# Nine of eleven gate/up chunks as seven products, in two stretches, with two sums of weights added by the loads

## The chip, the core and the metric

The kernel runs on one core of a Trainium2 chip. The metric is the device time of one execution in microseconds (us). TensorE (PE) multiplies matrices, VectorE (DVE) and ScalarE (ACT) work elementwise, GpSimd (POOL) and SyncE (SP) here issue DMAs. Each engine runs its own instructions strictly in order and waits on semaphores for the others.

## The reference

One layer on 256 tokens with 2048 channels, all in float32: a SwiGLU feed-forward, a mixer, a second feed-forward, each followed by a layer norm, and an embedding gate at the end.

```python
def _swiglu(x, w1, w3, w2):
    return (jax.nn.silu(x @ w1) * (x @ w3)) @ w2
...
x = _layer_norm(ALPHA * x + 0.5 * _swiglu(x, ffn1_w1[i], ffn1_w3[i], ffn1_w2[i]), ln1_g[i], ln1_b[i])
mix = _hybrid_mixer(x, w_in[i], ...)
x = _layer_norm(ALPHA * x + mix, ln2_g[i], ln2_b[i])
x = _layer_norm(ALPHA * x + 0.5 * _swiglu(x, ffn2_w1[i], ffn2_w3[i], ffn2_w2[i]), ln3_g[i], ln3_b[i])
x = x + jax.nn.sigmoid(x @ w_ple_gate[i]) * (p[i] @ w_ple_proj[i])
```

w1 and w3 are 2048 x 5632, w2 is 5632 x 2048. The mixer projects x by a wide matrix w_in, runs an mLSTM and a stick-breaking attention, and merges them under gates.

## The kernel before

**Matmuls.** A weight is loaded as a raw float32 tile of 128 partitions x 2 x 512 (256 rows by 512 columns, 512 KB). It is split in two: `hi` is the value rounded to the float32r type (a cast on ACT, L1243), `lo` is the rest (a subtraction on DVE, L1247). Activations are split in the same way. A unit is one split weight against one tile of 128 tokens: for each of the two blocks of 128 rows three matmuls of 512 columns, hi x hi, hi x lo and lo x hi (L1294 to L1296), six in all. They add up in one of eight PSUM banks; when the last unit of a sum has run, a function `done` or `add` evacuates the bank.

**Chunks.** The 5632 hidden columns are eleven chunks of 512. A plain chunk (`up`) has eight weights of w1 and eight of w3, each used by two units (the two token tiles). A chunk by `up7` goes through `seven`, a scheme of Strassen's kind: for each quad of 512 rows of the contraction, the activations form a 2 x 2 block matrix (two token tiles by two halves of the rows), and the weights another: B11 and B21 are the upper and lower half of the rows of w1, B12 and B22 those of w3. Seven products take the place of eight. M1 uses B11, M2 uses B21, M3 uses B22, M5 uses T1 = B11 + B12, M7 uses T3 = B12 + B22, M6 uses T2 = T1 + B22, M4 uses T4 = T2 + B21; the activations enter plainly or as sums that were made once (`act.forms`). Each product adds up over the four quads. Before the change, chunks 1, 2, 3, 5, 6, 7, 9 and 10 go this way, and 0, 4 and 8 plainly. All units of M1 run first, then all of M2 (each with its own load of B11 and B21), then for each quad M5, M7, M6, M4, M3. With `loaded` = 1, T1 is made by a load of B12 and an accumulating load of B11 into the same tile (issued by POOL, L1220), and T3 likewise in the last quad alone. The other sums are additions on DVE (L363).

In the mixer `both7` does the same for five pairs of column blocks of w_in, with `loaded` = 0: all sums on DVE.

**Order.** The program is a list of units. A main list (the plain chunks and the down passes, which multiply hidden chunks by w2 and add into the residual at L624) and a side list (the `up7` chunks) are merged by `weave` in proportion. From the list, weights are put in order of first use. `loads` issues raw loads on SP (L1215), at most 8 raw tiles held at once in the feed-forward (6 in the mixer's first part), and `split_one` splits a weight while at most 6 split weights are held. `make` puts the DVE additions shortly ahead of the split that needs them. An accumulating load's tile is moved three places ahead in the order of loads (AHEAD). Elementwise work after a product (`silu`, `late`, `turn`, which transposes hidden values for the down pass) is spawned with a delay counted in PE time. 48 pages of SBUF are shared by raw tiles, split tiles, activations and the residual.

Of the kernel before, what the change touches and what calls it, by code (L numbers as in the profile page):

```python
# [135 lines left out]
class Weight:  # L136


    def __init__(self, raw, loads, frees, make=None, after=None):
        self.raw, self.loads, self.frees, self.make, self.after = raw, loads, frees, make, after  # L140
        self.cols, self.uses, self.index, self.made = raw.cols, 0, None, False


class Unit:


    def __init__(self, tile, tt, acc, act, chunk, sub, start, stop, done):
        self.tile, self.cols, self.tt, self.acc = tile, tile.cols, tt, acc
        self.act, self.chunk, self.sub = act, chunk, sub
        self.start, self.stop, self.done = start, stop, done  # L150
        tile.uses += 1


# [34 lines left out]
def kernel(  # L188
# [159 lines left out]
    def seven(wa, ca, wb, cb, rows, cols, act, done, loaded):  # L348

        n = rows // (4 * P)
        accs = {m: {} for m in range(1, 8)}

        def unit(m, i, tile, src, half, sub):
            return Unit(tile, half, accs[m], src, i, sub, i == 0, i == n - 1, lambda ps, t, m=m: done(m, ps))

        def plus(out, a, b):
            def make():
                nc.vector.tensor_tensor(out=out.tile[:, :, :cols], in0=a.tile[:, :, :cols], in1=b.tile[:, :, :cols],  # L363
                                        op=ALU.add)
            return make

        units = []
        for m, sub in ((1, 0), (2, 2)):
            for i in range(n):
                units.append(unit(m, i, plain(rows_of(wa, (4 * i + sub) * P, ca, cols)), act, 0, sub))  # L370
        for i in range(n):
            b11, b12, b22, b21 = (rows_of(w, (4 * i + sub) * P, c, cols)
                                  for w, c, sub in ((wa, ca, 0), (wb, cb, 0), (wb, cb, 2), (wa, ca, 2)))
            by_load = loaded and i % loaded == 0
            if by_load:
                t1 = Raw(b12.src, cols, b11.src)
                first = Weight(t1, [t1], [])
            else:
                t1 = b11
                first = Weight(t1, [b11, b12], [], plus(b11, b11, b12))  # L380
            if loaded == 1 and i == n - 1:
                third = Weight(t3 := Raw(b12.src, cols, b22.src), [t3, b22], [t3])
            else:
                third = Weight(b12, [b12, b22] if by_load else [b22], [b12], plus(b12, b12, b22))
            units += [
                unit(5, i, first, act.forms, 0, 0),
                unit(7, i, third, act.forms, 1, 0),
                unit(6, i, Weight(t1, [], [], plus(t1, t1, b22), first), act.forms, 0, 2),
                unit(4, i, Weight(b21, [b21], [t1, b21], plus(b21, t1, b21)), act, 1, 2),
                unit(3, i, Weight(b22, [], [b22]), act.forms, 1, 2),  # L390
            ]
        return units

    def both7(w, ca, cb, act, dest, ready, loaded):

        r, held = {}, {}

        def put(k, t, a, b, op):
            nc.vector.tensor_tensor(out=r[k, t], in0=a, in1=b, op=op)

        def rest():
            u = r[0, 1]
            put(0, 1, held[7], u, ALU.add)
            z = r[1, 1] = dest(1, 1)
            nc.vector.scalar_tensor_tensor(out=z, in0=u, scalar=-1.0, in1=held[5],
                                           op0=ALU.mult, op1=ALU.subtract)
            ready(1, 1)
            return
            yield

        def done(m, ps):
            held[m] = ps
            if m == 1:
                r[0, 1] = dest(0, 1)
                nc.scalar.copy(r[0, 1], ps)
            elif m == 2:
                r[0, 0] = dest(0, 0)
                put(0, 0, ps, r[0, 1], ALU.add)
                ready(0, 0)
            elif m == 6:  # L420
                r[1, 0] = dest(1, 0)
                put(0, 1, ps, r[0, 1], ALU.add)
                put(1, 0, held[5], r[0, 1], ALU.add)
                sched.spawn(rest(), DELAY["rest"])
            elif m == 4:
                sched.until(lambda: (1, 1) in r)
                put(0, 1, ps, r[0, 1], ALU.add)
                ready(0, 1)
            elif m == 3:
                put(1, 0, ps, r[1, 0], ALU.subtract)  # L430
                ready(1, 0)

        return seven(w, ca, w, cb, D, COL, act, done, loaded)
# [110 lines left out]
    def ffn(w1, w3, w2, act, norm, skew=True, ahead=()):  # L544
# [22 lines left out]
        def up7(c):  # L567
            r, held = {}, {}

            def both(out, a, b, op):  # L570
                nc.vector.tensor_tensor(out=out, in0=a, in1=b, op=op)  # L571

            def done(m, ps):
                held[m] = ps
                if m == 1:
                    r["u"] = temp()
                    nc.scalar.copy(r["u"][:], ps)
                elif m == 2:
                    r["g0"] = temp()
                    both(r["g0"][:], ps, r["u"][:], ALU.add)  # L580
                    sched.spawn(silu(r["g0"]), DELAY["silu"])
                elif m == 6:
                    u, v, z = r["u"], temp(), temp()
                    both(u[:], ps, u[:], ALU.add)
                    both(v[:], held[5], u[:], ALU.add)
                    r["v"], r["z"] = v, z
                    sched.spawn(rest(), DELAY["rest"])
                elif m == 4:
                    sched.until(lambda: "rest" in r)
                    both(r["u"][:], ps, r["u"][:], ALU.add)  # L590
                    sched.spawn(silu(r["u"]), DELAY["silu"])
                elif m == 3:
                    both(r["v"][:], ps, r["v"][:], ALU.subtract)
                    sched.spawn(late(r["u"], r["v"], r["z"], r["g0"]), DELAY["late" if c < n - 1 else "last"])

            def rest():
                both(r["u"][:], held[7], r["u"][:], ALU.add)
# [466 lines left out]
    def ups(g, swap=False):  # L1064
# [3 lines left out]
            parts.reverse()  # L1068
        return parts[0] + parts[1]

    def gate_dest(g):
        def dest(k, t):
            if (g, t) not in gt:
                gt[g, t] = big()
            return gt[g, t][:, k * COL:(k + 1) * COL]
        return dest

    def pair(g):
        return both7(w_in, ga0 + g * COL, ga0 + D + g * COL, x1T, gate_dest(g), in_two(lambda t: gt[g, t], lambda k, t: ("gate", g, t, k)), 0)
# [6 lines left out]
    program.extend(weave(main, both7(w_in, sq0 + 2 * HS * DS, sq0 + 2 * HS * DS + COL, x1T, sv_dest, sv_ready, 0)  # L1086
                         + both7(w_in, 3072, 3072 + COL, x1T, mo_dest, mo_ready, 0) + pair(1) + pair(2) + pair(3)))
# [146 lines left out]
    def split_one():  # L1234
# [7 lines left out]
        for ks in pieces(j):  # L1242
# [3 lines left out]
                make(j + 2)  # L1246
            nc.vector.tensor_tensor(out=lo[:, ks], in0=r[:, ks], in1=hi[:, ks], op=ALU.subtract)  # L1247
# [28 lines left out]
    for u in program:  # L1276
# [14 lines left out]
        for k in range(2):  # L1291
            hi, lo = a[:, 0, u.sub + k], a[:, 1, u.sub + k]
            first, last = u.start and k == 0, u.stop and k == 1
            nc.tensor.matmul(ps, hi, w[0][:, k, :u.cols], start=first, stop=False)  # L1294
            nc.tensor.matmul(ps, hi, w[1][:, k, :u.cols], start=False, stop=False)  # L1295
            nc.tensor.matmul(ps, lo, w[0][:, k, :u.cols], start=False, stop=last)  # L1296
        sched.now += 6 * 0.2161 * u.cols / COL
        u.tile.uses -= 1
        if u.tile.uses == 0:
# [32 lines left out]
```

## Time and profile before

| | us |
|---|---|
| three runs | 2176.99, 2177.59, 2181.51 (median 2177.59) |
| the profiled execution, first to last instruction (span) | 2176.9 |

Stages of the profiled execution, about: 0 to 650 us first feed-forward and its norm, 700 to 1400 us mixer and second norm, 1400 to 2050 us second feed-forward, then the embedding gate. Busy share of the engines by slices of a fortieth of the span, in tenths, and what the DMA engines moved:

```profile
DVE  6899999999998799898988985799989999999874
ACT  7565665556664766667766563565656655656472
DMA  9899999899994666676878876589999999999743
GB/s 326 254 301 292 287 295 309 278 289 311 306 343 156 213 223 221 219 239 202 281 235 269 283 260 213 184 240 305 290 283 289 314 278 282 320 287 335 244 164 103
```

How to read it: a group's row names line, engine, operation, output and inputs, count, then busy time in us, the mean duration in ns, and the idle time of that engine just before these instructions with what ended it. PE's rows overlap each other, so the distance from start to start is what one matmul takes. A row of DMA issues gives the count, the size and the median time from issue to landing.

### The profile page before, as it was taken

The numbers are of one execution on the slowest core, as the hardware profiler recorded it, in microseconds if no ns is written. First come the engines' busy times: TensorE is split into PE (matmuls) and PEld (weight loads), VectorE is DVE, ScalarE is ACT, GpSimd is POOL, SyncE is SP. The second block draws the span as 40 slices with busy tenths as digits, with TensorE's granted clock in tenths as the row PEclk, the third lists the DMA queues.
The fourth block names the chain that finished last, engine by engine and source line by source line (L and its number), as shares of the span: only waits on it lengthen the run. The fifth ranks groups of instructions, "written<-read, shape, count | busy, mean of one in ns | idle before, by whom it ended". The sixth has DMA issues, their size and how long they took to land.

```text
span 2176.9 us, 28072 instructions
## 1 busy us (share of the span) xinstructions
PE 2167.6 (100%) x9846; PEld 1791.8 (82%) x9846; DVE 1936.8 (89%) x2123; ACT 1327.6 (61%) x1624; POOL 97.9 (4%) x88
## 2 busy tenths in 40 slices
PE   9999999999999999999999999999999999999999
PEld 7888888888888888888888888888888888888887
DVE  6899999999998799898988985799989999999874
ACT  7565665556664766667766563565656655656472
POOL 0000000000000000000000000000010001000000
PEclk9999999999999999999999999999999999999999
DMA  9899999899994666676878876589999999999743
GB/s 326 254 301 292 287 295 309 278 289 311 306 343 156 213 223 221 219 239 202 281 235 269 283 260 213 184 240 305 290 283 289 314 278 282 320 287 335 244 164 103
DMA packets 302221, 572.70 MB, mean 263 GB/s; under 512 B 18264, under 2 KB 35584, under 8 KB 302080
## 3 DMA queue, kind: packets, MB, share of 16 engines
q1 hardware_dynamic: 280320, 528.96, 71.5%
q0 software_dynamic: 21760, 41.95, 10.8%
q8 instruction: 77, 1.26, 0.2%
q14 instruction: 64, 0.52, 0.1%
HBM read 564.55 MB, written 6.29 MB: 262 GB/s over the span
## 4 chain that ended last, share of the span: by engine, by line
PE 97%; DMA 1%; DVE 1%; ACT 0%; issue 0%; SPq 0%; DVEq 0%
PE mm L1294 31%; PE mm L1296 31%; PE mm L1295 31%; PE ms L292 1%; DMA raw<-in_ffn_w_dram 1%; PE ms L498 0%; PE ms L989 0%; PE ms L887 0%; PE ms L965 0%; PE ms L902 0%; PE ms L978 0%; DVE split L1247 0%; ACT split L1243 0%; DMA big<-in_x_dram 0%; DMA raw<-in_w_up_m_dram 0%
## 5 line engine op out<-in xcount | busy, mean ns | idle before, releaser
L1243 ACT CAST split<-raw 128x1024 fp32r<-128x1024 f32 (+2 forms) x1065 | 1073.7, 1045 | 498.5 <-PE mm L1295 225.0
L1247 DVE TENSOR_TENSOR split<-raw,split 128x1024 fp32r<-128x1024 f32 (+2 forms) x1065 | 1255.9, 1209 | 91.4 <-ACT split L1243 75.9
L1294 PE MATMUL mm<-split,actT 128*128 128x512 f32 (+1 forms) x3080 | 1208.1, 392 | 1.5 <-DVE big L624 0.7
L1296 PE MATMUL mm<-split,actT 128*128 128x512 f32 (+1 forms) x3080 | 1194.2, 388 | 0.6 <-DVE actT L299 0.6
L1295 PE MATMUL mm<-split,actT 128*128 128x512 f32 (+1 forms) x3080 | 1192.6, 387 | 0.0
L1296 PEld LDWEIGHTS mm<-split,actT 128*128 128x128 f32 x3080 | 578.4, 188 | 122.1 <-DVE actT L299 1.4
L1294 PEld LDWEIGHTS mm<-split,actT 128*128 128x128 f32 x3080 | 578.8, 188 | 117.8 <-issue 1.3
L1295 PEld LDWEIGHTS mm<-split,actT 128*128 128x128 f32 x3080 | 579.1, 188 | 114.6 <-DVE split L1247 0.8
L363 DVE TENSOR_TENSOR raw<-raw 128x1024 f32<-128x1024 f32 x256 | 312.0, 1219 | 10.4 <-DMA raw<-in_ffn_w_dram 8.2
L1220 POOL DMA_DIRECT2D raw<-in_ffn_w_dram x80 | 95.5, 1193 | 1857.5 <-DVE temp L313 760.5
L294 ACT CAST actT<-ms 128x512 fp32r<-128x512 f32 x60 | 35.2, 588 | 110.6 <-PE ms L292 98.2
L571 DVE TENSOR_TENSOR temp<-mm,temp 128x512 f32<-128x512 f32 x112 | 76.8, 686 | 11.0 <-PE mm L1296 9.0
L624 DVE SCALAR_TENSOR_TENSOR big<-mm,big 128x512 f32<-128x512 f32 x96 | 65.3, 682 | 3.9 <-PE mm L1296 3.8
L299 DVE TENSOR_TENSOR actT<-ms,actT 128x512 fp32r<-128x512 f32 x60 | 40.8, 684 | 18.7 <-ACT big L298 9.8
L287 DVE TENSOR_TENSOR actT<-temp,actT 128x512 fp32r<-128x512 f32 x40 | 26.5, 686 | 17.3 <-ACT actT L286 17.2
L242 ACT ACTIVATE temp<-mm 128x512 f32<-128x512 f32 (+1 forms) x22 | 12.1, 559 | 47.0 <-PE mm L1296 47.0
L238 ACT ACT_TABLE_LOAD x31 | 39.8, 1283 | 0.5
L242 ACT ACTIVATE temp<-temp 128x512 f32<-128x512 f32 (+1 forms) x48 | 28.6, 595 | 10.0 <-DVE temp L571 10.0
L286 ACT CAST actT<-temp 128x512 fp32r<-128x512 f32 x40 | 24.1, 622 | 13.1 <-DVE temp L310 12.3
L1100 DVE SCALAR_TENSOR_TENSOR big<-big,mm 128x512 f32<-128x512 f32 x8 | 5.5, 685 | 25.3 <-PE mm L1296 25.3
L1157 DVE TENSOR_TENSOR temp<-temp,big 128x512 f32<-128x512 f32 (+1 forms) x10 | 5.8, 582 | 24.8 <-ACT temp L242 24.8
L242 ACT ACTIVATE temp<-ms,gbT 128x128 f32<-128x128 f32 x64 | 24.1, 460 | 5.5 <-PE ms L498 5.5
(131 smaller groups left out, 562.3 us busy)
## 6 DMA issues: line engine op xcount, KB each, us to landing
raw<-in_ffn_w_dram SPq DMA_DIRECT2D x655, 512.0 KB, 6.5
raw<-in_w_in_dram SPq DMA_DIRECT2D x184, 512.0 KB, 4.5
raw<-in_ffn_w_dram POOLq DMA_DIRECT2D x80, 512.0 KB, 9.4
raw<-in_w_out_dram SPq DMA_DIRECT2D x32, 512.0 KB, 5.8
raw<-in_w_ple_gate_dram SPq DMA_DIRECT2D x32, 512.0 KB, 5.4
raw<-in_w_in_dram SPq DMA_DIRECT2D x56, 256.0 KB, 3.4
raw<-in_w_up_m_dram SPq DMA_DIRECT2D x16, 512.0 KB, 5.0
raw<-in_w_up_sb_dram SPq DMA_DIRECT2D x16, 512.0 KB, 5.2
```

Source lines behind the costliest of these rows:

```text
L238: nc.scalar.preload_act_table_set(table[0])
L242: nc.scalar.activation(out, in_, func, **kw)
L299: nc.vector.tensor_tensor(out=dst[:, 1], in0=ps[:], in1=dst[:, 0], op=ALU.subtract)
L363: nc.vector.tensor_tensor(out=out.tile[:, :, :cols], in0=a.tile[:, :, :cols], in1=b.tile[:, :, :cols], op=ALU.add)
L571: nc.vector.tensor_tensor(out=out, in0=a, in1=b, op=op)
L624: nc.vector.scalar_tensor_tensor(out=xs, in0=ps, scalar=0.5, in1=xs, op0=ALU.mult, op1=ALU.add)
L1220: nc.gpsimd.dma_start(out=r.tile[:, :, :r.cols], in_=r.plus[0], accum_op=ALU.add)
L1243: nc.scalar.copy(hi[:, ks], r[:, ks])
L1247: nc.vector.tensor_tensor(out=lo[:, ks], in0=r[:, ks], in1=hi[:, ks], op=ALU.subtract)
L1294: nc.tensor.matmul(ps, hi, w[0][:, k, :u.cols], start=first, stop=False)
L1295: nc.tensor.matmul(ps, hi, w[1][:, k, :u.cols], start=False, stop=False)
L1296: nc.tensor.matmul(ps, lo, w[0][:, k, :u.cols], start=False, stop=last)
```

## The change

- Chunks 0 and 3 are plain; 1, 2 and 4 to 10 go by `up7`: nine in place of eight.
- Each chunk by seven products runs in two stretches over the quads. First M1, M5, M7, M6, M3 of each quad, with the M1 of the next quad ahead of M5; then M4 and M2 of each quad. Every raw tile is loaded once: B11 is read for M1, becomes T1 in place, then T2 and T4 in place, and is held to the second stretch; B21 is loaded there.
- M2 adds onto the bank in which M1 was summed, after M1 has been copied out. So M1 + M2 is there without an addition on DVE; in `up7` ACT takes its Silu straight from the bank, in `both7` ACT copies it.
- In the feed-forwards T1 and T3 of every quad are added by POOL's accumulating loads. T3: B12 is loaded and B22 added to it, as before in the last quad. T1: B12 is added onto B11's raw tile, issued right behind the two instructions that split it for M1 (`soon`).
- `in_line` puts the first M1 unit of a chunk four units ahead of the end of the chunk before it, in feed-forwards and mixer.
- The down passes take chunks (0), (1, 2), (3, 4), (5, 6), (7, 8), (9), (10) in place of (0), (1, 2), (3, 4, 5), (6, 8, 7), (9), (10).

```diff
@@ seven
         accs = {m: {} for m in range(1, 8)}
+        accs[2] = accs[1]
...
+        def plus_load(out, src):
+            def make():
+                nc.gpsimd.dma_start(out=out.tile[:, :, :cols], in_=src, accum_op=ALU.add)
+            return make
...
-        for m, sub in ((1, 0), (2, 2)):
-            for i in range(n):
-                units.append(unit(m, i, plain(rows_of(wa, (4 * i + sub) * P, ca, cols)), act, 0, sub))
...
+            m1 = Weight(b11, [b11], [])
+            if i in loaded[0]:
+                m5 = Weight(b11, [], [], plus_load(b11, b12.src[0]), m1)
+                m1.soon.append(m5)
             else:
+                m5 = Weight(b11, [b12], [], plus(b11, b11, b12), m1)
+            if i in loaded[1]:
+                b12.plus = b22.src
+                m7 = Weight(b12, [b12], [b12])
...
+            m6 = Weight(b11, [b22] if i in loaded[1] else [], [], plus(b11, b11, b22), m5)
+            m2 = Weight(b21, [], [b21])
+            m4 = Weight(b11, [b21], [b11], plus(b11, b11, b21), m6)
+            one.append(unit(1, i, m1, act, 0, 0))
+            rest.append([unit(5, i, m5, act.forms, 0, 0), unit(7, i, m7, act.forms, 1, 0),
+                         unit(6, i, m6, act.forms, 0, 2), unit(3, i, Weight(b22, [], [b22]), act.forms, 1, 2)])
+            then += [unit(4, i, m4, act, 1, 2), unit(2, i, m2, act, 0, 2)]
+            then[-1].onto = True
+        first = []
+        for i in range(n):
+            first += one[i + 1:i + 2] + rest[i]
+        return one[:1], first, then
+
+    def in_line(pairs):
+        out = []
+        for head, first, then in pairs:
+            at = max(len(out) - 4, 0)
+            out = out[:at] + head + out[at:] + first + then
+        return out
@@ up7, done
                 elif m == 2:
                     r["g0"] = temp()
-                    both(r["g0"][:], ps, r["u"][:], ALU.add)
-                    sched.spawn(silu(r["g0"]), DELAY["silu"])
+                    activate(r["g0"][:], ps, ACT.Silu)
+                    sched.spawn(late(r["u"], r["v"], r["z"], r["g0"]), DELAY["late" if c < n - 1 else "last"])
...
-            return seven(w1, c * COL, w3, c * COL, D, COL, act, done, 1)
+            return seven(w1, c * COL, w3, c * COL, D, COL, act, done, (range(4), range(4)))
@@ ffn
-        gate, hidden = zip(*(up(c) for c in (0, 4, 8)))
+        gate, hidden = zip(*(up(c) for c in (0, 3)))
...
-        main = flat(hidden[0] + gate[1] + down(0) + hidden[1] + gate[2] + down(1, 2) + hidden[2] + down(3, 4, 5)
-                    + down(6, 8, 7))
-        side = [u for c in (1, 2, 3, 5, 6, 7, 9, 10) for u in up7(c)]
+        main = flat(hidden[0] + gate[1] + down(0) + hidden[1] + down(1, 2) + down(3, 4) + down(5, 6) + down(7, 8))
+        side = in_line([up7(c) for c in (1, 2, 4, 5, 6, 7, 8, 9, 10)])
@@ split_one
         pos["split"] += 1
+        for f in w.soon:
+            f.make()
+            f.made = True
```

More of the change, by code (lines that the diff above doesn't have):

```diff
@@ L140, in __init__ @@
         self.raw, self.loads, self.frees, self.make, self.after = raw, loads, frees, make, after
-        self.cols, self.uses, self.index, self.made = raw.cols, 0, None, False
+        self.cols, self.uses, self.index, self.made, self.soon = raw.cols, 0, None, False, []
 class Unit:
@@ L365, in plus @@
             return make
-        units = []
-        for m, sub in ((1, 0), (2, 2)):
-            for i in range(n):
-                units.append(unit(m, i, plain(rows_of(wa, (4 * i + sub) * P, ca, cols)), act, 0, sub))
+        def plus_load(out, src):
+            def make():
+                nc.gpsimd.dma_start(out=out.tile[:, :, :cols], in_=src, accum_op=ALU.add)
+            return make
+        one, rest, then = [], [], []
         for i in range(n):
@@ L417, in done @@
                 r[0, 0] = dest(0, 0)
-                put(0, 0, ps, r[0, 1], ALU.add)
+                nc.scalar.copy(r[0, 0], ps)
                 ready(0, 0)
@@ L1069, in ups @@
         return parts[0] + parts[1]
+    none = ((), ())
     def gate_dest(g):
@@ L1293 @@
             first, last = u.start and k == 0, u.stop and k == 1
-            nc.tensor.matmul(ps, hi, w[0][:, k, :u.cols], start=first, stop=False)
-            nc.tensor.matmul(ps, hi, w[1][:, k, :u.cols], start=False, stop=False)
-            nc.tensor.matmul(ps, lo, w[0][:, k, :u.cols], start=False, stop=last)
+            nc.tensor.matmul(ps, hi, w[0][:, k, :u.cols], start=first, stop=False, skip_group_check=u.onto)
+            nc.tensor.matmul(ps, hi, w[1][:, k, :u.cols], start=False, stop=False, skip_group_check=u.onto)
+            nc.tensor.matmul(ps, lo, w[0][:, k, :u.cols], start=False, stop=last, skip_group_check=u.onto)
         sched.now += 6 * 0.2161 * u.cols / COL
```

32 lines of the change are left out of this document (9 added, 23 removed).

## The prediction, made before the changed kernel ran

> **What bounds the kernel now.** I read the page's first part, then who TensorE (PE) waited for, then the busy time by stretches, then the spacing of matmuls in one stretch.
>
> ```profile
> span 2176.9 us, 28072 instructions
> PE 2167.6 (100%) x9846; PEld 1791.8 (82%) x9846; DVE 1936.8 (89%) x2123; ACT 1327.6 (61%) x1624; POOL 97.9 (4%) x88
> ```
>
> PE is idle for 9.3 us of 2176.9. The view of waits, for PE from 40 to 2050 us, has four entries in all:
>
> ```profile
> PE mm L1294 <- DVE big L624: 0.7, 1, 0.7
> PE mm L1294 <- ACT big L242: 0.4, 1, 0.4
> PE mm L1294 <- DVE big L1049: 0.2, 1, 0.2
> PE ms L989 <- DVE temp L847: 0.2, 1, 0.2
> ```
>
> A matmul's "busy" overlaps its neighbours', so a busy PE alone does not prove a full one. The timeline does: start, duration, instruction.
>
> ```profile
> 600.07 0.39 PE L1295 MATMUL mm<-split,actT 128*128 128x512 f32 x1
> 600.30 0.40 PE L1296 MATMUL mm<-split,actT 128*128 128x512 f32 x1
> 600.53 0.39 PE L1294 MATMUL mm<-split,actT 128*128 128x512 f32 x1
> 600.77 0.39 PE L1295 MATMUL mm<-split,actT 128*128 128x512 f32 x1
> 600.99 0.39 PE L1296 MATMUL mm<-split,actT 128*128 128x512 f32 x1
> 601.22 0.60 PE L292 MATMUL ms<-ident,temp 128*128 128x128 f32 x4
> 601.58 0.48 PE L1294 MATMUL mm<-split,actT 128*128 128x512 f32 x1
> 601.90 0.39 PE L1295 MATMUL mm<-split,actT 128*128 128x512 f32 x1
> 602.12 0.40 PE L1296 MATMUL mm<-split,actT 128*128 128x512 f32 x1
> ```
>
> One starts every 0.23 us. More exactly, over 500 us of the first feed-forward stage (groups of PE, 100 to 600 us):
>
> ```profile
> L1294 PE MATMUL mm<-split,actT 128*128 128x512 f32 x724 | 283.4, 391 | 0.0
> L1296 PE MATMUL mm<-split,actT 128*128 128x512 f32 x724 | 281.9, 389 | 0.0
> L1295 PE MATMUL mm<-split,actT 128*128 128x512 f32 x724 | 281.7, 389 | 0.0
> L292 PE MATMUL ms<-ident,temp 128*128 128x128 f32 x68 | 10.2, 272 | 0.0
> ```
>
> Four transposes between two matmuls cost 602.12-600.99 less three steps, 0.45 us; 17 such blocks take 7.7 us, and 492.3 us over 2172 matmuls is 0.227 us each. So the order on PE sets the end, and a matmul taken out is worth 0.227 us as long as everything behind it keeps up. How near the others are, in the two woven feed-forward stages (columns: length, PE, PE weight loads, DVE, ACT, POOL, clock, DMA share, GB/s):
>
> ```profile
> 40.00:640.00 600.00, 600.00 (x2687) 496.73 (x2686) 564.23 (x558) 367.63 (x393) 47.76 (x40) 1.00 0.94 294
> 1440.00:2030.00 590.00, 589.31 (x2634) 487.58 (x2633) 552.58 (x537) 360.05 (x378) 45.38 (x39) 1.00 0.95 299
> ```
>
> Behind a full PE stand VectorE (DVE) at 94% and the DMA engines at 94 to 95%. The granted clock is 1.00.
>
> **The change, part by part.** *Products.* A gate/up chunk takes 2 weights x 8 loads x 2 token tiles x 6 = 192 matmuls plainly, and 4 quads x 7 products x 6 = 168 as seven products. Each feed-forward goes from 8 to 9 of 11 such chunks: 24 matmuls fewer, 48 in all, 48 x 0.227 = 10.9 us. The built order of the changed kernel has exactly 48 matmuls fewer on PE and as many transposes.
>
> *Vector and scalar work*, per feed-forward. Rows:
>
> ```profile
> L1243 ACT CAST split<-raw 128x1024 fp32r<-128x1024 f32 (+2 forms) x1065 | 1073.7, 1045 | 498.5 <-PE mm L1295 225.0
> L1247 DVE TENSOR_TENSOR split<-raw,split 128x1024 fp32r<-128x1024 f32 (+2 forms) x1065 | 1255.9, 1209 | 91.4 <-ACT split L1243 75.9
> L363 DVE TENSOR_TENSOR raw<-raw 128x1024 f32<-128x1024 f32 x256 | 312.0, 1219 | 10.4 <-DMA raw<-in_ffn_w_dram 8.2
> L571 DVE TENSOR_TENSOR temp<-mm,temp 128x512 f32<-128x512 f32 x112 | 76.8, 686 | 11.0 <-PE mm L1296 9.0
> L624 DVE SCALAR_TENSOR_TENSOR big<-mm,big 128x512 f32<-128x512 f32 x96 | 65.3, 682 | 3.9 <-PE mm L1296 3.8
> ```
>
> Split weights: a plain chunk has 16, a seven-product one 28, so +12 (DVE 12 x 1.209 = +14.5 us, ACT 12 x 1.045 = +12.5). Sums of weights on DVE: 11 a chunk become 8, since T1 and T3 are now both added by the load: 88 become 72, 16 x 1.219 = -19.5. Short operations on results: 9 in each of 8 chunks become 8 in each of 9, no change; the plain chunk's two multiplications go, -1.4. Down passes: 6 become 7, 8 more additions into the residual, 8 x 0.682 = +5.5. DVE together: -0.9 us, in a stage 5.45 us shorter: 563.3 of 594.5 us, 94.8% in place of 94.0%. ACT gains about 15 us on 368 (with three more table loads in the whole kernel); it has over 200 us free. Both are covered by PE; without that cover DVE would have 31 us to spare.
>
> *Loads.*
>
> ```profile
> q1 hardware_dynamic: 280320, 528.96, 71.5%
> q0 software_dynamic: 21760, 41.95, 10.8%
> raw<-in_ffn_w_dram SPq DMA_DIRECT2D x655, 512.0 KB, 6.5
> raw<-in_ffn_w_dram POOLq DMA_DIRECT2D x80, 512.0 KB, 9.4
> raw<-in_w_in_dram SPq DMA_DIRECT2D x184, 512.0 KB, 4.5
> ```
>
> A plain 512 KB load occupies the 16 engines for 0.715 x 2176.9 / (528.96/0.524) = 1.54 us, an accumulating one 0.108 x 2176.9 / 80 = 2.94 us. A seven-product chunk goes from 24 loads by SP and 5 accumulating by POOL to 16 and 8 (B11 and B21 are no longer read twice). Per feed-forward: 64 loads fewer by SP (-98.6 us) and 32 more by POOL (+94.1): -4.5 us in a stage 5.45 us shorter, so the share stays at 0.94 to 0.95. In the mixer 40 loads go (-62 us at 1.54), at a share where they were hidden: nothing. An accumulating load's price beside another one is not in the trace; below it cannot be under a plain load's 1.54, above I bound it by 5.9 (two in line). I take 2.94, since its 80 cases ran in these same stages.
>
> *The new wait.* T1 is now added into B11's own buffer: the load is queued on POOL only when M1's split has been read by ACT and DVE, and M5's split (ACT, then DVE, both in order) waits for its landing. Behind that split stand on ACT and DVE all later splits, the evacuation of finished products and the copies for transposes; PE waits for these. From the view of line L1220:
>
> ```profile
> L1220 POOL DMA_DIRECT2D raw<-in_ffn_w_dram x80: 1176/1189/1318, 50.1 to 1992.2; - x80
> DMA to landing us min/median/max: 5.7/9.4/13.2
> ```
>
> The order of the changed kernel puts 84 to 108 matmuls, mostly 96, between the point where M1's split is due and M5's first product (12 of 69 cases at 84, one at 72). 96 are 21.8 us, 84 are 19.1. The chain needs the split twice (1.05+1.21 each) and a landing: 13.9 us at the median, 17.7 at the longest, 18.9 with another POOL issue of 1.19 ahead of it. So PE is just covered, by 5 to 8 us mostly and by 0.2 at worst. I put 1.5 us on what still gets through (0.1 us at each tight quad), with 0 and 24 us (the rival below) as ends.
>
> The Trainium skill, DMA: Bandwidth & Descriptors, section SWDGE vs HWDGE vs iDMA, says that only one software queue is allocated and that each DMA engine takes turns between it and the hardware queues. By that rule T1 would stand in line behind the T3 of the same quad, which the order issues just ahead of it, and land near the 13.2 of the row above rather than 9.4: 17.7 us for the chain. In the trace of before POOL's loads come 15 us apart, so no run here shows two in line.
>
> *Look-ahead.* Raw tiles stay limited to 8, and up to four B11 are now held through a chunk. In the order, the shortest distance from a load to its weight's first product falls from 78 to 66 matmuls (15.0 us) in the feed-forwards, in 12 loads each (one of them 60), and from 69 to 48 (10.9 us) in the mixer. Landing 6.5 and a split 2.3 make 8.8 of 15.0; in the mixer 4.5 and 2.3 make 6.8 of 10.9. Hidden, hence nothing. B11's sums, M2's move to the same accumulator as M1 and the ACT copies in the mixer (5 x 0.6 us) move work without adding to PE.
>
> **Sum.** 2176.9 - 10.9 + 1.5 = 2167.5 us for a profiled execution. The median shown is 2177.59, 0.7 above the span; so 2168.
>
> **The rivals.**
>
> *A, slower: T1 lands late and DVE runs out of room.* The splits of M1 and M5 are due 60 matmuls apart, 13.6 us; M1's split and a landing take 2.3 + 9.4 = 11.7, but 2.3 + 13.2 = 15.5 where T1 queues behind T3: 1.9 us late, and DVE stands still. DVE's room is 31 us a feed-forward, 0.86 us for each of 36 quads; beyond that PE waits. Price: 72 x (d - 0.86). With d = 1.2: +24 us, 2192; with all 1.9: 2243. For it: POOL's queue and DVE at 94.8%. Against: PE's cover of 5 us, and that DVE is often still busy when ACT's part of a split ends, so part of d is no idle time:
>
> ```profile
> DVE split L1247 <- ACT split L1243: 14.2, 21, 1.5
> ```
>
> (DVE's waits from 100 to 600 us; only 14 us of 500.) Chance 0.17.
>
> *B, no change: the shorter look-ahead takes the gain back.* All raw loads from 100 to 600 us landed so (min/median/max):
>
> ```profile
> DMA to landing us min/median/max: 3.4/7.0/13.7
> ```
>
> At 13.7 a load with 15.0 us is late by 13.7 + 2.3 - 15.0 = 1.0 us. Were nine of the 24 such, PE would lose 9 us: 2177. Against: the longest come when queues are full, and fewer SP loads are now in flight. Chance 0.12.
>
> *C, slower: the DMA engines become the bound.* Their room is 5 to 6% of 594 us, some 31, plus the 4.5 saved. 72 accumulating loads use that up at 2.94 + 35.5/72 = 3.43 us each. At 3.6 the stage is 12 us longer, twice: 2168 + 24 = 2192. Chance 0.05.
>
> *That it doesn't do what it says* is excluded for PE (48 matmuls are gone from its order); what stays of that is B.
>
> **How the numbers follow.** Forecast 0.66 at 2168 (2164 to 2173 by itself), A 0.17, B 0.12, C 0.05. The low end is the full 10.9 us with PE's last idle 2 us in the middle of the kernel also gone, 2164, less 1 for the measurement; the high end is A and C at 2192, beyond which I leave about 0.1. Within 0.2% (2173.2 to 2181.9, about what a measurement of this kernel can tell from no change) lies B. Faster 0.66, same 0.13, slower 0.21.
>
> **What would show it.** Right: 9192 matmuls of the three lines at 0.227 us, PE waits still a few us, DVE about 563 us in each woven stage, POOL 144 issues, HBM bytes down by 54 MB. Against me: an entry of PE waiting for splits, or ACT's splits waiting for raw tiles by tens of us in total (A); landings of POOL's loads well over 9.4 (A, C); a DMA share of 0.99 or more with PE idle in the woven stages (C); PE gaps in the mixer, 700 to 1200 us (B).

## The result, and the profile after

The changed kernel takes 2194.11 us (median of four runs, 2191.28 to 2202.03); before, in the same series, 2179.4 (2176.99 to 2181.51). The ratio on record is 1.0076, with an interval of 1.0058 to 1.0094 (the two medians alone give 1.0067): slower, where 2168 was forecast. The profiled execution was the slowest of the four, so the losses read from it are some 8 us larger than the median's.

The page after: engines, DMA queues and DMA issues.

```profile
span 2200.3 us, 27579 instructions
PE 2169.1 (99%) x9798; PEld 1786.9 (81%) x9798; DVE 1927.1 (88%) x2122; ACT 1345.9 (61%) x1658; POOL 175.0 (8%) x152
...
q0 software_dynamic: 39168, 75.51, 19.3%
...
raw<-in_ffn_w_dram SPq DMA_DIRECT2D x527, 512.0 KB, 6.3
raw<-in_ffn_w_dram POOLq DMA_DIRECT2D x144, 512.0 KB, 9.1
```

The work is what was planned: 48 matmuls fewer on PE, DVE 10 us less busy, 144 accumulating loads. Yet PE is idle for 2200.3 - 2169.1 = 31.2 us in place of 9.3, and its busy time rose by 1.5 where 48 steps of 0.227 should have taken 10.9 off it: 12.4 us went into slower steps. 21.9 us more of idle time and 1.5 of busy time make the 23.4 us between the two spans.

Where PE is idle, by stretches (columns as in the prediction): the two feed-forwards and the mixer after, then the mixer before.

```profile
40.00:640.00 600.00, 591.58 (x2632) 486.81 (x2631) 550.12 (x551) 364.39 (x397) 85.03 (x71) 1.00 0.93 261
1440.00:2030.00 590.00, 582.41 (x2580) 479.26 (x2579) 538.56 (x534) 355.75 (x381) 82.72 (x70) 0.99 0.93 260
700.00:1400.00 700.00, 693.82 (x3237) 573.84 (x3236) 596.16 (x737) 447.67 (x637) 0.00 (x0) 1.00 0.62 201
```

```profile
700.00:1400.00 700.00, 699.02 (x3266) 577.83 (x3265) 602.46 (x746) 449.46 (x645) 0.00 (x0) 1.00 0.71 232
```

PE lost 8.4 and 7.6 us in the feed-forwards (0 and 0.7 before) and 6.2 in the mixer (1.0 before). DVE and the DMA engines are less busy there than before, not more: on average neither has come nearer to its limit.

Who waited for what, in the view of waits of the changed kernel (total us, times, longest); first ACT and DVE, then PE:

```profile
ACT split L1261 <- DMA raw<-in_ffn_w_dram: 162.2, 60, 8.2
DVE split L1265 <- ACT split L1261: 135.5, 105, 4.8
```

```profile
PE ms L292 <- DVE actT L299: 8.6, 6, 3.2
PE mm L1316 <- DVE split L1265: 5.2, 6, 1.4
PE ms L292 <- DVE big L641: 3.7, 2, 2.0
PE ms L981 <- DVE actT L1011: 3.6, 1, 3.6
```

Of ACT's 162.2 us for raw tiles, nearly all is for T1, as the view of T1's loads (L371) says under "who waited for it":

```profile
L371 POOL DMA_DIRECT2D raw<-in_ffn_w_dram x72: 1183/1198/1705, 52.2 to 2003.5; - x72
...
  ACT split L1261: 159.5, 58
...
DMA to landing us min/median/max: 5.6/9.7/12.6
```

So 58 of 72 T1 came too late for ACT, by 2.75 us on average. But PE waited little for splits (5.2 us, of which 2.5 in the two feed-forwards); it waited mostly at transposes (`ms`, L292 and L981) for a PSUM bank that DVE had not emptied yet (12.2 us in the feed-forwards). One such place, in the timeline of POOL, ACT, DVE and PE:

```profile
1717.29 1.19 POOL L1238 DMA_DIRECT2D raw<-in_ffn_w_dram  x1 [8.63 <-DMA raw<-in_ffn_w_dram]
1718.47 1.24 POOL L371 DMA_DIRECT2D raw<-in_ffn_w_dram  x1
...
1719.32 2.95 ACT L1261 CAST split<-raw 128x1024 fp32r<-128x1024 f32 x3 [4.10 <-DMA raw<-in_ffn_w_dram]
...
1730.39 1.05 ACT L1261 CAST split<-raw 128x1024 fp32r<-128x1024 f32 x1 [3.51 <-DMA raw<-in_ffn_w_dram]
...
1725.15 5.76 DVE L1265 TENSOR_TENSOR split<-raw,split 128x1024 fp32r<-128x1024 f32 x5
1731.47 1.23 DVE L1265 TENSOR_TENSOR split<-raw,split 128x1024 fp32r<-128x1024 f32 x1 [0.57 <-ACT split L1261]
1732.62 0.68 DVE L641 SCALAR_TENSOR_TENSOR big<-mm,big 128x512 f32<-128x512 f32 x1
...
1730.95 0.39 PE L1317 MATMUL mm<-split,actT 128*128 128x512 f32 x1
1733.36 0.66 PE L292 MATMUL ms<-ident,temp 128*128 128x128 f32 x4 [2.01 <-DVE big L641]
```

POOL waits 8.63 us for B12 to land, issues T3's addition, and right behind it, at 1718.47, T1's, which lets ACT go at 1730.39, 11.9 us later. ACT has stood still for 4.10 us (for the T1 before) and then 3.51; DVE is behind by then, works off five splits in a row and waits for the sixth; the evacuation L641, which stands behind that split in DVE's order, comes at 1732.62, and the four transposes that need its bank stop PE for 2.0 us. What PE missed here was not T1's product but an evacuation behind T1's split. In the whole trace 67 of the 72 T1 were issued while another accumulating load had not landed, and 20 of them directly behind T3's issue on POOL.

A stall has a second price. The granted clock (the column before the DMA share) in the stretches of four stalls and behind them:

```profile
283.50:286.80 3.30, 1.21 (x8) 0.75 (x8) 1.83 (x2) 2.98 (x4) 0.00 (x0) 0.99 1.08 313
286.80:290.20 3.40, 3.40 (x10) 2.63 (x9) 2.58 (x3) 1.53 (x2) 0.00 (x0) 0.50 0.80 157
354.60:362.00 7.40, 7.36 (x35) 6.18 (x36) 7.40 (x8) 4.94 (x6) 0.00 (x0) 1.00 1.04 255
1126.40:1129.80 3.40, 3.15 (x9) 2.61 (x10) 1.57 (x3) 1.50 (x3) 0.00 (x0) 0.51 0.46 150
1802.30:1809.10 6.80, 5.87 (x16) 4.81 (x17) 5.57 (x7) 3.64 (x5) 0.00 (x0) 0.50 0.77 200
```

After a stall of 2.5 us from start to start (283.5) PE ran at half clock for 3.4 us; likewise behind the one of 2.4 us at 1731 and the one of 4.0 at 1122.7, and for 6.8 us behind one of 3.6 at 1799.7. After 2.0 us (at 352.6) it did not. That is 17.0 us at half clock, about 8.5 us of the 12.4 in slower steps. The remaining 3.9 are not placed; part of them is that each wait of PE hides some 0.16 us of its length in the busy time, since a matmul counts as busy for 0.39 us and the next is due after 0.23. Before, no such stretch exists in the middle of the kernel.

The mixer has its own stall, the one at 1122.7. Timeline of DVE, ACT and PE there:

```profile
1119.21 2.35 DVE L1265 TENSOR_TENSOR split<-raw,split 128x1024 fp32r<-128x1024 f32 x2
1121.48 2.35 DVE L365 TENSOR_TENSOR raw<-raw 128x1024 f32<-128x1024 f32 x2
1123.75 2.35 DVE L1265 TENSOR_TENSOR split<-raw,split 128x1024 fp32r<-128x1024 f32 x2
1126.02 0.48 DVE L1011 TENSOR_TENSOR actT<-ms,actT 128x128 fp32r<-128x128 f32 x2
...
1122.79 1.05 ACT L1261 CAST split<-raw 128x1024 fp32r<-128x1024 f32 x1 [2.27 <-DVE raw L365]
...
1126.65 1.62 PE L981 MATMUL ms<-big 128*128 128x256 f32 x4 [3.61 <-DVE actT L1011]
```

DVE is never idle in it. Two splits, two sums and two splits stand ahead of L1011, which takes part in emptying the bank that PE needs; ACT, whose copy of the same bank (L1009) is also due, first waits 2.27 us for a sum.

### The profile page after: what moved, and what is told of

It is laid out like the page before. It is cut to its first block, busy times and chain, and to the rows that moved or that the text cites. A ratio compares the mean times of both kernels' runs of the same rounds, so it can differ in the third digit from the quotient of the medians.

```text
span 2200.3 us, 27579 instructions
## 1 busy us (share of the span) xinstructions
PE 2169.1 (99%) x9798; PEld 1786.9 (81%) x9798; DVE 1927.1 (88%) x2122; ACT 1345.9 (61%) x1658; POOL 175.0 (8%) x152
## 5 line engine op out<-in xcount | busy, mean ns | idle before, releaser
L1261 ACT CAST split<-raw 128x1024 fp32r<-128x1024 f32 (+1 forms) x1089 | 1087.0, 1043 | 562.0 <-DVE raw L365 240.8
L1265 DVE TENSOR_TENSOR split<-raw,split 128x1024 fp32r<-128x1024 f32 (+1 forms) x1089 | 1275.5, 1209 | 139.7 <-ACT split L1261 135.5
L1315 PE MATMUL mm<-split,actT 128*128 128x512 f32 x3064 | 1204.4, 393 | 2.5 <-DVE big L417 1.4
L1316 PE MATMUL mm<-split,actT 128*128 128x512 f32 x3064 | 1190.2, 388 | 5.3 <-DVE split L1265 5.2
L1317 PE MATMUL mm<-split,actT 128*128 128x512 f32 x3064 | 1190.6, 389 | 0.6 <-DVE actT L299 0.6
L365 DVE TENSOR_TENSOR raw<-raw 128x1024 f32<-128x1024 f32 x224 | 271.6, 1218 | 8.5 <-DMA raw<-in_ffn_w_dram 7.3
L1238 POOL DMA_DIRECT2D raw<-in_ffn_w_dram x72 | 86.8, 1205 | 1566.8 <-DVE big L548 750.3
L371 POOL DMA_DIRECT2D raw<-in_ffn_w_dram x72 | 94.8, 1317 | 214.9 <-DVE split L1265 186.5
L294 ACT CAST actT<-ms 128x512 fp32r<-128x512 f32 x60 | 35.0, 586 | 79.5 <-PE ms L292 68.6
L641 DVE SCALAR_TENSOR_TENSOR big<-mm,big 128x512 f32<-128x512 f32 x112 | 76.2, 682 | 3.1 <-PE mm L1317 2.9
L299 DVE TENSOR_TENSOR actT<-ms,actT 128x512 fp32r<-128x512 f32 x60 | 40.8, 683 | 15.7 <-ACT big L298 11.1
L242 ACT ACTIVATE temp<-mm 128x512 f32<-128x512 f32 (+1 forms) x36 | 20.4, 572 | 51.9 <-PE mm L1317 51.9
L292 PE MATMUL ms<-ident,temp 128*128 128x128 f32 x176 | 27.4, 279 | 12.3 <-DVE actT L299 8.6
L292 PEld LDWEIGHTS ms<-ident,temp 128*128 128x128 f32 x176 | 21.2, 142 | 21.2 <-DVE actT L299 11.6
```

The source lines that it names most:

```text
L292: nc.tensor.transpose(ps[:, k], src[:, k * P:(k + 1) * P], ident[:])
L371: nc.gpsimd.dma_start(out=out.tile[:, :, :cols], in_=src, accum_op=ALU.add)
L641: nc.vector.scalar_tensor_tensor(out=xs, in0=ps, scalar=0.5, in1=xs, op0=ALU.mult, op1=ALU.add)
L1238: nc.gpsimd.dma_start(out=r.tile[:, :, :r.cols], in_=r.plus[0], accum_op=ALU.add)
L1261: nc.scalar.copy(hi[:, ks], r[:, ks])
```

## The experiments

The theory after the result was rival A: T1 lands late, because it stands behind T3. Its rivals were the load that 72 more accumulating transfers put on the DMA engines, the shorter look-ahead, and the mixer's new order. Three groups of runs follow; in brackets is the median of the kernel before in the same group. These three agree within 0.5 us, so medians are also compared across groups. The changed kernel itself ran in the first series only.

**First group (2178.19): one part away at a time.**

`m1_two_ahead` gives T1 a quad more time: the M1 units run two quads ahead.

```diff
-            first += one[i + 1:i + 2] + rest[i]
-        return one[:1], first, then
+            first += one[i + 2:i + 3] + rest[i]
+        return one[:2], first, then
```

> M1 of each quad stands two quads ahead of its M5 in place of one: mostly 126 to 150 matmuls between the point where M1's split is due and M5's first product, in place of 96. Same matmuls, loads and sums; one more B11 tile is held of the eight raw tiles, so plain loads start later. Theory A (T1, added onto B11 behind M1's split, lands after M5's split is due; ACT, DVE and the freeing of PSUM banks stand still behind it, and PE with them): ACT's waits for raw tiles fall from 162 us to under 30, PE's idle time to about 10 us, and the time to 2166 to 2172. Theory B (the shorter look-ahead of the plain loads): it grows worse, 2200 or more. Theory C (the DMA engines are the bound): no change, 2190 to 2198.

2255.34 us, ratio 1.0357 (1.0316 to 1.0397): far slower, as theory B had it. Two rows of its waits:

```profile
PE ms L292 <- DVE actT L299: 41.5, 12, 5.8
...
DVE raw L365 <- DMA raw<-in_ffn_w_dram: 79.5, 35, 5.5
```

ACT now waits for T1 32.7 us in place of 159.5, so the extra time reached T1. But one more B11 is held, which leaves one raw tile fewer for the loads of B21 and B22: DVE's sums wait for these 79.5 us (7.3 in the changed kernel), and PE's stalls grow to 6.2 us, with 14 stretches of half clock. A's remedy thus ran into the mechanism behind rival B, and the run doesn't separate the two.

`t1_left_out` drops T1's load and its wait, `t3_left_out` drops T3's.

```diff
-                m5 = Weight(b11, [], [], plus_load(b11, b12.src[0]), m1)
-                m1.soon.append(m5)
+                m5 = Weight(b11, [], [], None, m1)
```

> T1's 72 accumulating loads are left out: M5 takes B11 alone, so part of the sums is not computed. All matmuls stay. Theory A: 2166 to 2170, ACT hardly waits for raw tiles. Theory C: the 72 loads at 2.94 us give back 106 us of the DMA engines in each feed-forward, so faster too, 2166 to 2172; only the run without T3's additions tells A from C. Theory B: little change, 2188 or more, since the plain loads start where they did.

```diff
-                b12.plus = b22.src
```

> T3's 72 accumulating loads are left out: M7 takes B12 alone, so part of the sums is not computed. As many accumulating loads go as in the run without T1's, but T1's wait stays. Theory A in its plain form (the wait of M5's split behind M1's split): most of the loss stays, 2183 to 2192, with ACT waiting over 100 us for raw tiles. A with the queue (T1 late because T3 stands ahead of it in POOL's queue): 2166 to 2174. Theory C: as fast as the run without T1's additions.

2172.58 us without T1 (0.9973; 0.9962 to 0.9983), 2174.9 without T3 (0.9981; 0.9971 to 0.9991). The first feed-forward in the two profiles, the first row without T1, the second without T3:

```profile
40.00:640.00 600.00, 600.00 (x2687) 496.81 (x2686) 564.99 (x564) 373.93 (x405) 41.68 (x35) 1.00 0.82 237
```

```profile
40.00:640.00 600.00, 600.00 (x2686) 496.81 (x2685) 564.69 (x565) 372.99 (x404) 42.99 (x36) 1.00 0.83 237
```

PE is full in both, so either half of the pair is harmless alone; the first is 2.6 us above theory A's range, the second 0.9 above that of A with the queue and 8 below that of A in its plain form, and the mixer is as changed in both (its own cost follows below). Without T3, T1 is still added in place and still waited for, 66.5 us in 28 cases, and it lands after 8.2 us (median) and 10.8 at most: waits of this number and length don't reach PE. But each of these kernels also moves less, a DMA share of 0.82 to 0.84 in place of 0.93, so queue and load are still mixed.

`mixer_old` leaves the feed-forwards as changed and gives the mixer its former order.

```diff
@@ both7
-                nc.scalar.copy(r[0, 0], ps)
+                put(0, 0, ps, r[0, 1], ALU.add)
...
-        return seven(w, ca, w, cb, D, COL, act, done, loaded)
+        return seven_old(w, ca, w, cb, D, COL, act, done, loaded)
```

> The five pairs of the mixer go back to the order of before (all M1, then all M2, each with its own loads; M2 added on DVE), the feed-forwards stay as changed. The trace of the changed kernel shows PE stalls of 1.5, 4.0 and 1.8 us between 830 and 1180 us and a clock of 0.5 for 3.4 us behind the longest. If those come from the mixer's new order: 2184 to 2189, and no halved clock near 1126 us. If they are chance or come from elsewhere: 2190 to 2197.

2190.96 us (1.0049; 1.003 to 1.0068), with a spread from 2183 to 2194. Most of the loss stays: the feed-forwards carry it. By its median this lies in the range given for a mixer that costs nothing. But in its profile (of the fastest of the six runs) no stretch of half clock is left and PE works 699.07 of the 700 us from 700 to 1400, as before the change. With runs of this kernel 11 us apart, and of the changed kernel too, 3 us between their medians can't tell the mixer's cost; `ffn_old` below can.

**Second group (2178.45): queue or load, and the mixer alone.**

`t3_out_copies` leaves T3's accumulation out, and SP moves two other 512 KB blocks for each, so that the engines' load comes back without POOL's queue.

```diff
+                for _ in range(2):
+                    nc.sync.dma_start(out=copies[k], in_=r.extra[0])
```

> As the run without T3's additions (M7 takes B12 alone, so part of the sums is not computed), and for each addition left out SP issues two plain copies of 512 KB inside the device memory, which nobody waits for. The DMA engines then have about the load of the changed kernel again, but POOL's queue holds T1's loads alone. Queue theory (T1 is late because T3's accumulating load stands just ahead of it in POOL's queue): no loss comes back, 2172 to 2178, and T1's loads land as fast as without the copies. Load theory (all loads land late because the DMA engines are full): the loss comes back, 2186 to 2200, and plain loads land later too.

2181.36 us (1.0014; 1.0004 to 1.0024), at a DMA share of 0.94 to 0.95. T1's loads (L372 in this kernel):

```profile
  ACT split L1267: 107.0, 44
...
DMA to landing us min/median/max: 6.0/9.2/11.1
```

It stands between: of the 19.2 us that T3's absence was worth, the copies take back 6.5. T1 lands 1.0 us later than without them (median 8.2), so load alone delays it too; its longest landing is 11.1 us, where the changed kernel has 12.6. The copies are not quite T3's load: they also write to the device memory, and SP's loads for the feed-forwards land after 6.8 us, in place of 5.3 without them and 6.3 in the changed kernel. So 6.5 is a rough figure for the load.

`t1_first` keeps everything and only swaps the two on POOL: T3's load is held back and issued right behind the next T1, or earlier where its own split comes near.

```diff
             if r.plus is not None:
-                nc.gpsimd.dma_start(out=r.tile[:, :, :r.cols], in_=r.plus[0], accum_op=ALU.add)
+                held_back.append(r)
...
         for f in w.soon:
             f.make()
             f.made = True
+            let_go()
```

> The changed kernel with one difference: on POOL the accumulating load of T3 is issued right behind the next T1 in place of ahead of it. Same loads, sums and matmuls. Queue theory: T1 lands 2 to 3 us sooner and T3 later, which had 5 to 6 us to spare; ACT's waits for raw tiles fall from 162 us to under 80, PE's stalls in the feed-forwards mostly go, 2174 to 2182 (the mixer's own stalls stay). Load theory: both land late as before, 2190 to 2198.

2180.53 us (1.0011; 1.0002 to 1.0021), 13.6 us better by the medians than the changed kernel, with the same transfers. T1's loads in this run:

```profile
L371 POOL DMA_DIRECT2D raw<-in_ffn_w_dram x72: 1176/1185/1206, 51.5 to 1988.1; - x72
...
  ACT split L1270: 74.3, 31
...
DMA to landing us min/median/max: 6.1/8.9/10.3
```

T1's longest landing falls from 12.6 to 10.3 us and ACT's wait for it from 159.5 to 74.3. The expectation that ACT's whole wait for raw tiles would fall below 80 us was missed: it is 200.8, since T3 now lands later (11.9 median, 8.9 before the swap) and ACT waits 107.4 us for it. That wait costs PE little: with 204.4 us of such waits PE is full but for 1 us in each feed-forward of `t1_first_mixer_old` below. So T1's place behind T3 is the larger part of the loss, and the sum of ACT's waits is no measure of it. The swap changes two things at once, the order in the DMA queue and that POOL no longer holds T1's issue until B12 has landed for T3; it doesn't tell them apart.

`ffn_old` has the feed-forwards as before and the mixer as changed (the diff is against the kernel before).

```diff
@@ both7
-        return seven(w, ca, w, cb, D, COL, act, done, loaded)
+        return seven_new(w, ca, w, cb, D, COL, act, done, loaded)
-    program.extend(weave(main, both7(w_in, sq0, ...)
+    program.extend(weave(main, in_line([both7(w_in, sq0, ...)
```

> The feed-forwards go back to the order and the counts of before (eight of eleven chunks by seven products), the mixer's five pairs stay as changed. Theory that the mixer's new order costs by itself (in both runs that left additions out PE stalled for 1.5, 4.0 and 1.8 us in it, and the clock was halved for 3.4 to 6.8 us): 2182 to 2186, that is 5 to 7 us over the kernel before, with the same three stalls. Theory that they only show under the changed feed-forwards: 2177 to 2179.

2184.96 us (1.0027; 1.0017 to 1.0037): the mixer's new order costs 6.5 us by itself. PE's time from 700 to 1400 us, and its longest wait, the stall shown above under this kernel's line numbers:

```profile
700.00:1400.00 700.00, 693.79 (x3235) 573.40 (x3235) 595.04 (x733) 449.73 (x643) 0.00 (x0) 1.00 0.65 199
PE ms L1029 <- DVE actT L1059: 3.6, 1, 3.6
```

`t1_first_mixer_old` joins the swap with the old mixer.

> T3's accumulating load behind T1's, and the mixer's pairs in the order of before. If queue theory and the mixer's own cost both hold, the full count shows: 2167 to 2173, faster than the kernel before by 0.2 to 0.5%. If either falls: 2176 or more.

2174.7 us (0.9982; 0.9973 to 0.9991), no stretch of half clock, PE 599.02 of 600 and 589.17 of 590 us busy in the feed-forwards (in the profile of its fastest run, 2171.48; the slowest took 2177.84). The time lies between the two ranges: faster than before, but 2 us short of the full count.

**Third group (2178.68): room for raw tiles and look-ahead.** Three of these start from `t1_first_mixer_old`, `two_ahead_raw9` from `m1_two_ahead`. A ninth raw tile in the feed-forwards, for `two_ahead_raw9` and for `t1f_mo_raw9`:

```diff
-HELD = {"ffn": (8, 6), ...
+HELD = {"ffn": (9, 6), ...
```

> M1 two quads ahead, as in the run that took 2255, but nine raw tiles may be held in the feed-forward in place of eight. In the order the shortest distance from a plain load to its product goes from 60 back to 66 to 72 matmuls, the median from 78 to 90. Look-ahead theory (that run was slow because the extra B11 tile put off the loads of B22 and B21: DVE's sums waited 79.5 us for raw tiles): 2185 to 2210, DVE's waits for raw tiles under 30 us, and PE's stall at the end of each chunk mostly gone. Rival (two M1 splits at the end of the chunk before overload DVE there): stays at 2240 or more.

2225.29 us (1.0207; 1.0191 to 1.0222): a ninth raw tile takes back 30 of the 77 us by which `m1_two_ahead` was slower than before, and DVE's sums wait 61.9 us for loads in place of 79.5. Neither theory's range held it. The stalls at the ends of chunks stay in number (12 waits of L292 for L299), with 26.8 us in place of 41.5.

> T3's load behind T1's, the mixer in the order of before, and nine raw tiles held in the feed-forward in place of eight. Plain loads have 72 to 90 matmuls in place of 60 to 78 up to their product, T3's 132 in place of 120. If what is left over the full count (2174.7 against 2167.5) is waits for raw tiles: 2167 to 2171, ACT's waits for raw tiles from 204 us to under 80. If the ninth tile takes a page that the split tiles lack: 2175 or more.

With the ninth tile, `t1f_mo_raw9` takes 2172.26 us (0.997; 0.9958 to 0.9981): faster than both kernels. It lies between the two ranges again, and ACT's waits for raw tiles, which were to fall below 80 us, are 182.9. Whether the ninth tile gains anything is not shown: the intervals of this run and of `t1_first_mixer_old` overlap, and PE is as busy in both profiles. PE's largest entry in the view of waits is 1.4 us in four waits, for splits. Its first feed-forward:

```profile
40.00:640.00 600.00, 598.90 (x2676) 494.89 (x2675) 562.04 (x563) 371.01 (x403) 85.64 (x71) 1.00 0.95 267
```

`t1f_mo_two_first` holds one B11 more at the chunk's start only:

```diff
-            first += one[i + 1:i + 2] + rest[i]
+            first += (one[1:3] if i == 0 else one[i + 2:i + 3]) + rest[i]
```

> T3's load behind T1's, the mixer in the order of before, and the second and third M1 of a chunk both ahead of its first M5. T1 has 102 to 108 matmuls up to its product in place of 84 to 96, the end of the chunk before is left as it was. If T1's rest of a wait matters (ACT waited 76 us for it): 2169 to 2173. If the look-ahead matters more, since one more B11 is held through the first quads: 2176 to 2190.

2222.14 us (1.0202; 1.0188 to 1.0216), slower than either side had it.

```profile
DVE raw L365 <- DMA raw<-in_ffn_w_dram: 81.1, 31, 6.7
```

The same row as in `m1_two_ahead` (34.5 us in `t1_first_mixer_old`), here with the end of the chunk before left as it was: with a raw tile held a quad longer, the sums wait longer for their loads.

`t1f_mo_ahead4` moves T3's tile four places ahead in the order of loads in place of three (`AHEAD = 4`).

> T3's load behind T1's, the mixer in the order of before, and T3's tile moved four places ahead in the order of loads in place of three: T3 has 132 to 138 matmuls up to its product in place of 120 to 126, the plain loads keep 60 to 78. If T3's own wait (the larger part of ACT's 204 us) is what is left: 2169 to 2173. If it is covered anyway: 2173 to 2177.

2185.45 us (1.0036; 1.0022 to 1.0049), 10.7 us worse than with three, outside both ranges. Two rows of its waits:

```profile
DVE raw L365 <- DMA raw<-in_ffn_w_dram: 26.8, 23, 2.7
PE ms L292 <- DVE big L687: 5.4, 2, 3.2
```

The sums wait less for loads here than with three places (26.8 us, 34.5 there), so the scarcity of raw tiles seen in `t1f_mo_two_first` doesn't show in this row. PE again waits at transposes for evacuations; why they come late here is open.

## Why the prediction was wrong, point by point

- **Products.** Right. 48 matmuls went, at 0.227 us each. `t1_left_out` has the mixer's 6.5 us and no wait for T1's load: 2178.2 - 10.9 + 6.5 = 2173.8 by the prediction's term, 2172.58 measured.
- **Vector, scalar and DMA work.** Right in that nothing here became the bound. DVE's busy time fell by 9.7 us and ACT's rose by 18.3 in the whole kernel; the sums for the two feed-forwards alone gave -1.8 and about +30. HBM traffic fell by 54.5 MB (54 forecast). An accumulating load took 0.193 x 2200.3 / 144 = 2.95 us of the 16 engines (2.94 taken); the DMA share was 0.93, so C, the engines as the bound, didn't happen. As contention the load counts for roughly 6.5 us, by the copies.
- **The new wait: the step that failed.** The prediction asked whether T1's chain ends before T1's own product is due, found 5 to 8 us of cover, and put 1.5 us on the rest. That comparison was about right: in the feed-forwards PE waited 2.5 us for splits, in the slowest of the four runs. (One case of the order, at 72 matmuls or 16.3 us, was not covered at the longest landing, against "0.2 at worst".) But the same paragraph names the evacuations and the copies for transposes that stand behind the late split on ACT and DVE, and no cover was worked out for them. They were due earlier than T1's product, and PE stalled there for 12.2 us in the two feed-forwards, most of the loss seen in them, besides the half clock behind the stalls. Where 1.5 us was put, the swap puts 13.6 on T1's place behind T3 alone.
- **Two in line.** The prediction says that in the trace of before POOL's loads come 15 us apart, so that no run shows two in line. The median is 13.2 us, and 16 of the 80 were issued while another had not landed. They landed after 11.5 us (median; 9.7 to 13.2), the other 64 after 9.1 (5.7 to 11.5). One pair, in the timeline of POOL and in the view of L1220 from 399 to 401 us:

```profile
399.10 2.44 POOL L1220 DMA_DIRECT2D raw<-in_ffn_w_dram  x2 [14.98 <-PE mm L1296]
DMA to landing us min/median/max: 10.5/11.8/13.2
```

So the lateness of a load in line, the ground of rival A, could be read before the change ran.

- **The look at DVE's idle time against A.** "Only 14 us of 500" described a kernel without the in-place addition. After the change ACT waits 159.5 us for T1, and DVE 39.8 us for ACT's splits from 40 to 640 us, in place of 14.9.
- **Rival A.** It had T1 landing late behind T3, and at 2192 nearly the time, at a chance of 0.17. The Trainium skill, DMA: Bandwidth & Descriptors, section SWDGE vs HWDGE vs iDMA (only one software queue), was the rule that spoke against the forecast. The swapped order agrees with it: T1's longest landing 10.3 us in place of 12.6, T3's median 11.9 in place of 8.9. A's price did not follow its formula, though, so that its time came out near was partly luck. DVE's waits for ACT's splits in the two feed-forwards rose from 14.9 + 16.9 to 39.8 + 46.8 us, by 54.8 or 0.76 for each of 72 quads: less than the 0.86 us of room, which by the formula costs nothing. The lateness is uneven (the longest of these waits is 4.8 us), and PE loses where a bank is emptied late, not by the stage's average. And part of the 26 us came from elsewhere:
- **The mixer.** "B11's sums, M2's move ... move work without adding to PE" was wrong: 6.5 us by `ffn_old`, 5.8 by the step from `t1_first` to `t1_first_mixer_old`. In the code, M5's sum was formerly made from a B11 loaded for it; now it is made in B11's one tile and can't start until M1's split has been read. The timeline shows sums and splits piled ahead of an evacuation; that the sum in place piled them is argued from the code, not tested. Which of the mixer's edits does it (the sum in place, the five ACT copies, the first unit moved) was not tried one by one.
- **A stall's price.** The prediction counted a stall once. In the profile 17.0 us at half clock lie behind four stalls.
- **Look-ahead.** Right for this order: landings of SP's loads were 6.3 us, and the sums waited 7.3 us for loads. But it had little room. One tile more, held for a quad, cost 47 us (`t1f_mo_two_first` against `t1_first_mixer_old`). A place more for T3 cost 10.7, for a reason that stays open.
- **The signs.** "ACT's splits waiting for raw tiles by tens of us" appeared and was right for A. "Landings well over 9.4" did not: the median is 9.1, and T1's lateness shows only in its own view. "PE gaps in the mixer" appeared too, but not for B's reason: its largest is the evacuation behind sums and splits.

Put together from the medians: the changed kernel 2194.1; T1 ahead of T3 on POOL 2180.5; with the old mixer 2174.7; with a ninth raw tile 2172.3. The last step is within the noise. The forecast of 2168 is 4 us below that. In the profile of `t1f_mo_raw9` PE is idle 10.8 us (9.3 before) and spends 3.2 us more than the forecast's steps, without half clock and with no wait over 1.1 us; no run took this apart. Open too is what, beyond the tiles, costs the kernels with M1 two quads ahead their stalls at the chunk's end, and how exactly the loss divides between T1's place in the queue and the engines' load.

## What to carry to other kernels

When an addition is moved into a load that must wait for a reader, work out the cover of everything that stands behind that wait on the in-order engines, the evacuations first, and not only of the product that uses the result. Of two accumulating loads in one queue, issue first the one that is due first. Where raw tiles are scarce, holding one longer can put off other loads, so a remedy that buys time with a tile can cost more than the wait.

## What the runs showed of the hardware

- In the changed kernel PE stalls of 2.4 us or more, from start to start, were followed by 3.4 us (once 6.8) at a granted clock of 0.5; stalls of 2.1 us or less were not. The other runs show that the length alone doesn't decide: a stall of 2.89 us in `m1_two_ahead` (at 508.6) and one of 3.29 us in `two_ahead_raw9` (at 1825.6) were followed by full clock, while in `t1f_mo_two_first` two of 1.48 and 1.93 us close together (at 1950.9 and 1953.5) came with 6.8 us at 0.5. The Trainium skill, TensorE: Matmul & The Clock Gate, section HAM oscillation, has gaps of over some 3.4 us as what must be avoided; here shorter ones sufficed.
- An accumulating load issued while another was under way landed later: in the trace of before after 11.5 us (median of 16) in place of 9.1 (median of 64).
- POOL's issue of an accumulating load took 1.18 to 1.20 us in the median (before 1.189, T1 in `t1_first` 1.185). Directly behind another it shows up to 1.7 (T1 in the changed kernel 1.705 at most), but then its record starts up to 0.5 us before the one ahead ends.
